# First FFN layer by seven block products in place of eight, with its output stored in DRAM

## Chip, cores and metric

One core of a Trainium2 chip runs the whole program. The metric is the device time of one execution in microseconds, as the median of several runs. The engines are TensorE (PE, matmuls; its weight loads are PEld), VectorE (DVE), ScalarE (ACT), GpSimd (POOL) and SyncE (SP, which issues most transfers). Sixteen DMA engines move the data.

## What is computed

One layer of a hybrid encoder for 1024 prompt tokens and 8 × 16 sample tokens, 1152 rows of 1024 in all. Three mixers come first; the change touches only the end of the layer:

```python
def _merge_and_ffn(x, o_a, o_b, o_c, gate_logits, w_out, ln1_g, ln1_b, w_ff1, b_ff1, w_ff2, b_ff2, ln2_g, ln2_b):
    ...
    h = _layer_norm(DN_ALPHA * x + merged @ w_out, ln1_g, ln1_b)
    f = jnp.square(jax.nn.relu(h @ w_ff1 + b_ff1)) @ w_ff2 + b_ff2
    return _layer_norm(DN_ALPHA * h + f, ln2_g, ln2_b)
```

`w_ff1` is 1024 × 4096 and `w_ff2` 4096 × 1024, all in float32.

## The kernel before

Every float32 product is made of three matmuls: each operand is split into a rounded upper part and the rest (`xh`/`xl` for the activations, `whi`/`wlo` for weights, `uh`/`ul` for the hidden layer, `h2`/`l2`, here also `h`/`l`, for the second weights), and the three products upper × upper, upper × rest and rest × upper are added in PSUM. `split` (L168, L169) makes the two parts: POOL rounds (or ACT, where asked), DVE subtracts. All matmuls are issued at L115.

`phase_out` holds what concerns us. A first loop over nine token tiles of 128 adds the out-projection to the residual, normalises (`layer_norm`, whose last addition of 1024 elements is POOL's, L1319), transposes the result on PE (tile `tp`, PSUM tag t, two banks) and writes it split into `xh` (ACT, L1241) and `xl` (DVE, L1242): feature on the partitions, 8 blocks `k` of 128 features by 1152 tokens. The normalised rows themselves stay in SBUF in nine tiles `acc0` to `acc8`, which later collect the output.

Then the FFN runs in 16 blocks of two hidden tiles `f` of 128. For each `f`, 72 matmuls of 128 × 384 (8 blocks `k`, 3 parts, 3 token chunks) fill PSUM tag g (tile `ps`); ACT takes relu and square (L1263, L1264), and the result is split into `uh` and `ul`, three buffers each. The second layer of the block takes 108 matmuls of 128 × 512 (9 token tiles, 2 halves, 6 each) into tag o (tile `op`, three banks), and DVE adds each bank to its half of an `acc` tile (L1289). After the second block POOL adds the bias `b_ff2` (L1296). The program's order is written as a loop, but a scheduler fixes each engine's own order when the program is built: it puts the first-layer matmuls of one block among the second-layer ones of the block before. At run time each engine works its queue strictly in that order and waits on semaphores. The weights come over SP's queue (`wraw`, `w2raw`).

Of the kernel before, what the change touches and what calls it, by code (L numbers as in the profile page):

```python
# [11 lines left out]
F32 = mybir.dt.float32  # L12
F32R = mybir.dt.float32r
AF = mybir.ActivationFunctionType
ALU = mybir.AluOpType
# [4 lines left out]
P = 128  # L20
D = 1024
# [3 lines left out]
NT = SEQ + DB * DT  # L25
CW = 384
NCH = NT // CW
KT = D // P
MEM = 256
FF = 4096  # L30
NF = FF // P
# [3 lines left out]
ALPHA = 2.0 ** 0.25  # L35
# [22 lines left out]
def run(g, n=-1):  # L58

    while n and next(g, g) is not g:  # L60
        n -= 1


class K:
# [66 lines left out]
    def setup(self):  # L131
        nc, d = self.nc, self.d
        nc.scalar.preload_act_table_set("natural_log_exp_and_others")
        cst = self.const.tile([P, C_END], F32, name="cst")
        self.cst = cst
        self.ident = cst[:, C_ID:C_ID + P]
        self.og = self.dram.tile([KT, P, NT], F32, name="og")
        self.started = set()

        self.gates = [(0, 0), (0, 1), (0, 2), (0, 3), (1, 7)] + [(2, t) for t in range(4)] + [(a, t) for t in range(4, KT) for a in (0, 2)]  # L140
        self.oa, self.oc, self.gb = (self.dram.tile([KT, P, NT], F32, name=n) for n in ("oa", "oc", "gb"))
        self.spq = self.dram.tile([KT, P, NT], F32, name="spq")
        self.spk = self.dram.tile([KT, P, NT], F32, name="spk")
        self.spn = self.dram.tile([2, KT, P, NT], F32, name="spn")
        self.rows = self.dram.tile([2, 8, 9, P], F32, name="rows")
        self.b_dram()
        eps = self.const.tile([P, 4], F32, name="eps")
        nc.vector.memset(eps[:, 0:1], 1e-6)
        nc.vector.memset(eps[:, 1:2], 1e-5)
        nc.vector.memset(eps[:, 2:3], float(np.log(128.0 ** -0.5)))  # L150
        nc.vector.memset(eps[:, 3:4], 1.0)
        self.eps = eps
        self.sums = self.const.tile([P, NT // P, 2], F32, name="sums")
# [1053 lines left out]
    def phase_out(self, pool, ps):  # L1207
        nc, d = self.nc, self.d
        T9 = NT // P
        hh, hl = self.xh, self.xl  # L1210
        accs = [pool.tile([P, D], F32, name=f"acc{i}") for i in range(T9)]
        with self.pool("p2a") as pa:
            for i in range(6):
                nc.scalar.copy(accs[i][:, 0:512], self.early[i])
                nc.sync.dma_start(accs[i][:, 512:D], d["x"][i][:, 512:D])
# [13 lines left out]
            for i in range(T9):  # L1229
# [2 lines left out]
                run(self.out_mm(i, 1, w1, o, accs[i][:, 512:D]))  # L1232
                a = accs[i]
                self.layer_norm(pa, a, self.sums[:, i, :], lng, hl[:, :, t])
                for u in range(2):
                    tp = ps.tile([P, 512], F32, name="tp", tag="t", bufs=2)
                    for k in range(4):
# [4 lines left out]
                    nc.vector.tensor_sub(hl[:, s, t], v, hh[:, s, t].bitcast(F32))  # L1242
        self.right.close()
        with self.pool("p2b") as pb:
            bf = pb.tile([P, NF], F32, name="bf")
            nc.sync.dma_start(bf, d["b_ff1"])
            lng = pb.tile([P, 2, D], F32, name="lng")
            bf2 = pb.tile([P, D], F32, name="bf2")
            for t, n in ((bf2, "b_ff2"), (lng[:, 0, :], "ln2_g"), (lng[:, 1, :], "ln2_b")):
                nc.sync.dma_start(t, d[n].broadcast_to([P, D]))  # L1250
            blk = 2
            for f0 in range(0, NF, blk):
                hid = []
                for f in range(f0, f0 + blk):
                    w = self.weights(d["w_ff1"][f].rearrange("p (k c) -> p k c", k=KT))
                    uh = pb.tile([P, NT], F32R, name="uh", bufs=3)
                    ul = pb.tile([P, NT], F32R, name="ul", bufs=3)
                    for c in range(NCH):
                        n = slice(c * CW, (c + 1) * CW)
                        p = self.psg.tile([P, 512], F32, name="ps", tag="g")  # L1260
                        run(self.gemm(p[:, :CW], w, hh, hl, c * CW, (c + 1) * CW))
                        r = pb.tile([P, CW], F32, name="r", bufs=2)
                        nc.scalar.activation(r, p[:, :CW], AF.Relu, bias=bf[:, f:f + 1])  # L1263
                        nc.scalar.activation(r, r, AF.Square)  # L1264
                        self.split(uh[:, n], ul[:, n], r)
                    w2 = []
                    for u in range(2):
                        raw = pb.tile([P, 512], F32, name="w2raw", bufs=3)
                        nc.sync.dma_start(raw, d["w_ff2"][f][:, u * 512:(u + 1) * 512])
                        h2 = pb.tile([P, 512], F32R, name="h2", bufs=6)  # L1270
                        l2 = pb.tile([P, 512], F32R, name="l2", bufs=6)
                        self.split(h2, l2, raw)
                        w2.append((h2, l2))
                    hid.append((uh, ul, w2))
                last = f0 + blk == NF
                for i in range(T9):
                    t = slice(i * P, (i + 1) * P)
                    for u in range(2):
                        o = ps.tile([P, 512], F32, name="op", tag="o", bufs=3)
                        m = 0  # L1280
                        for uh, ul, w2 in hid:
                            for a, b in ((uh, w2[u][0]), (uh, w2[u][1]), (ul, w2[u][0])):
                                self.mm(o, lhsT=a[:, t], rhs=b, start=m == 0, stop=m == 3 * blk - 1)
                                m += 1
                        a = accs[i][:, u * 512:(u + 1) * 512]
                        if f0 == 0:
                            nc.vector.scalar_tensor_tensor(a, a, ALPHA, o, op0=ALU.mult, op1=ALU.add)
                        elif not last:
                            nc.vector.tensor_add(a, o, a)  # L1289
                        else:  # L1290
                            if u == 0:
                                sm = pb.tile([P, 2], F32, name="sm", bufs=2)
                            nc.vector.tensor_tensor_reduce(out=a, in0=o, in1=a, scale=1.0, scalar=0.0, op0=ALU.add, op1=ALU.add, accum_out=sm[:, u:u + 1])  # L1293
                    a = accs[i]
                    if f0 == blk:
                        nc.gpsimd.tensor_add(a, a, bf2)  # L1296
                    if last:
                        self.layer_norm(pb, a, sm, lng, hl[:, :, t], i >= T9 - 2)
                        m = 2 if i >= T9 - 2 else 1
                        for u in range(m):  # L1300
                            v = slice(u * D // m, (u + 1) * D // m)
                            nc.sync.dma_start(d["o_y"][i][:, v], a[:, v])

    def layer_norm(self, pool, a, s, gb, jk, short=False):

# [99 lines left out]
```

## Time and profile before

| what | value |
|---|---|
| median of 3 runs | 2823.54 us (2819.36 to 2833.57) |
| the profiled execution | 2831.98 us, its span 2830.2 us |
| busy in the span | PE 2685.3, DVE 1460.4, ACT 1008.4, POOL 819.5 us |
| mean granted clock of PE | 0.976 |

The profiled execution is one run among several, and the trace's times are those of that run. Busy is the time in which an engine has an instruction under way; a matmul is shown with its whole pipeline, so that two neighbours overlap, and the distance of two starts is what one costs. The FFN stands from about 2010 us to the end of the span.

### The profile page before, as it was taken

How to read it: one execution, taken by the hardware profiler on the slowest of the kernel's cores; microseconds unless marked ns; L12 is line 12 of the kernel's file. 1: busy time of each engine (PE TensorE's matmuls, PEld its weight loads, DVE VectorE, ACT ScalarE, POOL GpSimd, SP SyncE). 2: the span in 40 equal slices, each digit the busy share in tenths (PEclk: the TensorE clock that was granted, in tenths of full speed). 3: DMA queues.
4: the chain of work that ended last, by engine and by line, in shares of the span. 5: the costliest groups of instructions: out<-in, count | busy, mean ns of one | idle time of the engine just before them, and what ended most of it. 6: DMA issues, size and time to landing. Idle time of an engine off the chain costs nothing.

```text
span 2830.2 us, 45047 instructions
## 1 busy us (share of the span) xinstructions
PE 2685.3 (95%) x16361; PEld 2486.4 (88%) x16361; DVE 1460.4 (52%) x3353; ACT 1008.4 (36%) x2749; POOL 819.5 (29%) x1197
## 2 busy tenths in 40 slices
PE   8989999989899989999989898999999999999997
PEld 7979899989899988998878888888989899998986
DVE  4646474737375655333366557554544444444445
ACT  4636363736364544222423333233411111111113
POOL 2222132212122221122355555432342121121212
PEclk9999999999999999999989999999999999999999
DMA  7252524333333424344676676654201011110101
GB/s 254 76 172 79 174 86 174 119 124 125 121 130 129 155 91 158 136 164 151 189 207 191 192 209 199 189 161 144 71 30 60 30 52 38 38 53 30 52 27 67
DMA packets 263006, 343.27 MB, mean 121 GB/s; under 512 B 54704, under 2 KB 178240, under 8 KB 258752
## 3 DMA queue, kind: packets, MB, share of 16 engines
q1 hardware_dynamic: 201344, 245.93, 27.7%
q10 hardware_dynamic: 61440, 94.46, 9.5%
q8 instruction: 129, 2.11, 0.3%
q14 instruction: 93, 0.76, 0.1%
HBM read 235.18 MB, written 105.13 MB: 120 GB/s over the span
## 4 chain that ended last, share of the span: by engine, by line
PE 51%; DMA 8%; DVE 4%; issue 3%; POOL 1%; ACT 1%; SPq 0%; DVEq 0%; ACTq 0%; POOLq 0%
PE ps L115 26%; PE op L115 15%; PE t L115 3%; PE S L115 1%; PE sc L115 1%; PE kk L115 1%; DMA wraw<-in_w_mem 1%; DVE tmp L775 1%; PE o L115 1%; PE tb L120 1%; DMA bv<-spn 1%; PE ob L115 1%; PE od L115 1%; DMA o_akp<-y 1%; DMA og<-gt 1%
## 5 line engine op out<-in xcount | busy, mean ns | idle before, releaser
L115 PE MATMUL ps<-xh,whi 128*128 128x384 f32 x2712 | 958.1, 353 | 31.4 <-ACT y L313 13.9
L115 PE MATMUL ps<-xl,whi 128*128 128x384 f32 x2712 | 935.6, 345 | 0.0
L115 PE MATMUL ps<-xh,wlo 128*128 128x384 f32 x2712 | 933.5, 344 | 0.9 <-DVE wlo L169 0.9
L115 PEld LDWEIGHTS ps<-xh,whi 128*128 128x128 f32 x2712 | 517.7, 191 | 50.3 <-ACT y L313 14.5
L115 PEld LDWEIGHTS ps<-xl,whi 128*128 128x128 f32 x2712 | 517.4, 191 | 14.1 <-issue 2.9
L115 PEld LDWEIGHTS ps<-xh,wlo 128*128 128x128 f32 x2712 | 515.9, 190 | 10.2 <-issue 3.9
L168 POOL TENSOR_SCALAR whi<-wraw 128x512 fp32r<-128x512 f32 x261 | 180.6, 692 | 513.6 <-PE ps L115 414.8
L1289 DVE TENSOR_TENSOR acc<-op,acc 128x512 f32<-128x512 f32 x252 | 174.2, 691 | 276.1 <-PE op L115 276.0
L1263 ACT ACTIVATE r<-ps,bf 128x384 f32<-128x384 f32 x96 | 55.7, 581 | 664.7 <-PE ps L115 664.7
L169 DVE TENSOR_TENSOR wlo<-wraw,whi 128x512 fp32r<-128x512 f32 x261 | 195.2, 748 | 185.0 <-POOL whi L168 179.0
L115 PE MATMUL op<-h,uh 128*128 128x512 f32 x576 | 225.6, 392 | 1.2 <-DVE sm L1293 1.2
L115 PE MATMUL op<-h,ul 128*128 128x512 f32 x576 | 226.1, 392 | 0.0
L115 PE MATMUL op<-l,uh 128*128 128x512 f32 x576 | 225.5, 392 | 0.0
L371 POOL TENSOR_SCALAR pt<-pt,sta 128x640 f32<-128x640 f32 (+3 forms) x144 | 114.1, 793 | 293.5 <-DVE sta L370 242.5
L168 POOL TENSOR_SCALAR uh<-r 128x384 fp32r<-128x384 f32 x96 | 55.5, 578 | 492.0 <-ACT r L1264 480.1
L367 DVE CUSTOM_DVE_ANT_0 pt<-S,tab 128x640 f32<-128x640 f32 (+4 forms) x128 | 83.9, 656 | 122.8 <-PE S L115 85.6
L607 DVE SCALAR_TENSOR_TENSOR y<-z,wc,y 128x384 f32<-128x384 f32 (+1 forms) x216 | 128.7, 596 | 17.5 <-ACT y L604 15.5
L115 PEld LDWEIGHTS op<-h,ul 128*128 128x128 f32 x576 | 108.2, 188 | 23.9
L115 PEld LDWEIGHTS op<-h,uh 128*128 128x128 f32 x576 | 108.2, 188 | 19.5 <-DVE sm L1293 2.0
L115 PEld LDWEIGHTS op<-l,uh 128*128 128x128 f32 x576 | 108.1, 188 | 15.5
L369 ACT ACTIVATE pt<-pt,sta 128x640 f32<-128x640 f32 (+3 forms) x144 | 101.4, 705 | 49.4 <-DVE sta L368 35.7
L169 DVE TENSOR_TENSOR ul<-r,uh 128x384 fp32r<-128x384 f32 x96 | 53.7, 560 | 102.2 <-POOL uh L168 102.2
(374 smaller groups left out, 4600.5 us busy)
## 6 DMA issues: line engine op xcount, KB each, us to landing
wraw<-in_w_in SPq DMA_DIRECT2D x160, 256.0 KB
kb<-in_cak SPq DMA_DIRECT2D x16, 1024.0 KB
vb<-in_cav SPq DMA_DIRECT2D x16, 1024.0 KB
o_aks<-kb ACTq DMA_DIRECT2D x16, 1024.0 KB
wraw<-in_w_ff SPq DMA_DIRECT2D x64, 256.0 KB
w2raw<-in_w_ff SPq DMA_DIRECT2D x64, 256.0 KB
o_avs<-vb ACTq DMA_DIRECT2D x16, 992.0 KB
spn<-kn ACTq DMA_DIRECT2D x48, 192.0 KB
```

The lines of the kernel that those rows point to most:

```text
L115: ins = self.nc.tensor.matmul(out, **kw)
L120: ins = self.nc.tensor.transpose(out, **kw)
L168: nc.gpsimd.tensor_scalar(hi, raw, 1.0, 0.0, op0=ALU.mult, op1=ALU.add)
L169: nc.vector.tensor_sub(lo, raw, hi.bitcast(F32))
L367: nc.vector.tensor_tensor_reduce(out=P_, in0=S, in1=tab, scale=1.0, scalar=-3e38, op0=ALU.add, op1=ALU.max, accum_out=st[:, 0:1])
L369: nc.scalar.activation(P_, P_, AF.Exp, bias=st[:, 1:2], accum_out=st[:, 2:3])
L371: nc.gpsimd.tensor_scalar(P_, P_, st[:, 3:4], 0.0, op0=ALU.mult, op1=ALU.add)
L607: nc.vector.scalar_tensor_tensor(y[:, :w], z[:, i:i + w], wc[:, i:i + 1], y[:, :w], op0=ALU.mult, op1=ALU.add)
L775: nc.vector.tensor_tensor(tmp[:, 0:t, 0:t], y[:, 0:t, 0:t], m[:, 0:t, t].unsqueeze(1).broadcast_to([72, t, t]), op=ALU.mult)
L1263: nc.scalar.activation(r, p[:, :CW], AF.Relu, bias=bf[:, f:f + 1])
L1289: nc.vector.tensor_add(a, o, a)
```

## The change

The first layer is written as a 2 × 2 block product, h cut into two halves of features and two of tokens, and `w_ff1` into two halves of features and two neighbouring tiles `f`. One level of the Strassen–Winograd scheme takes seven products in place of eight. Its operands on the activation side are four sums (S1, S2, S4 in new tiles `s1h` to `s4l`; S3 over the part of `xh`/`xl` that is no longer wanted), made once after the first loop; on the weight side four sums per pair of tiles (`tsum`, on POOL). The seven results are put together by DVE adds into tiles `keep`. The tiles f = 0 and 1 are still done directly, with 384 columns; the 15 pairs after them have matmuls of 288 columns, 24 per product.

The hidden layer goes to a DRAM buffer `hid`, the normalised rows to `hd`, and the second layer is a loop of its own, `ffn2`, which reads both back. It does its rounding to `uh` on ACT.

```diff
@@ phase_out
-        accs = [pool.tile([P, D], F32, name=f"acc{i}") for i in range(T9)]
         with self.pool("p2a") as pa:
+            accs = [pa.tile([P, D], F32, name=f"acc{i}") for i in range(T9)]
...
                 self.layer_norm(pa, a, self.sums[:, i, :], lng, hl[:, :, t])
+                nc.scalar.dma_start(self.hd[i], a)
...
         with self.pool("p2b") as pb:
...
+            self.ffn1(pb, ps)
+        with self.pool("p2c") as pb:
+            self.ffn2(pb, ps)
+
+    def ffn1(self, pool, ps):
...
+        S = [tuple(pool.tile([P, 4, H], F32R, name=f"s{i}{n}") for n in "hl") for i in (1, 2, 4)]
+        S.insert(2, (hh[:, top, two], hl[:, top, two]))
+        for k in range(4):
...
+            tmp = lambda: pool.tile([P, H], F32, name="sum", bufs=5)
+            s1, s2, s3, u, v = (tmp() for _ in range(5))
+            nc.vector.tensor_add(s1, a21[0], a22[0])
+            nc.gpsimd.tensor_add(u, a21[1], a22[1])
+            nc.vector.tensor_add(s1, s1, u)
+            nc.gpsimd.tensor_sub(s3, a11[0], a21[0])
+            nc.gpsimd.tensor_sub(v, a11[1], a21[1])
+            nc.vector.tensor_add(s3, s3, v)
+            nc.vector.tensor_sub(s2, s1, a11[0])
+            nc.vector.tensor_sub(s2, s2, a11[1])
+            self.cast(S[0], k, s1)
+            self.cast(S[2], k, s3)
+            self.cast(S[1], k, s2)
+            nc.vector.tensor_sub(s2, a12[0], s2)
+            nc.vector.tensor_add(s2, s2, a12[1])
+            self.cast(S[3], k, s2)
...
+        for f in range(2, NF, 2):
...
+            t1, t2, t3, t4 = (pool.tile([P, 4, P], F32, name="tsum", bufs=6) for _ in range(4))
+            nc.gpsimd.tensor_sub(t1, R[0, 1], R[0, 0])
+            nc.gpsimd.tensor_sub(t2, R[1, 1], t1)
+            nc.gpsimd.tensor_sub(t3, R[1, 1], R[0, 1])
+            nc.gpsimd.tensor_sub(t4, R[1, 0], t2)
...
+            names = iter("tgotgot")
+            def product(a, raw):
+                w = [self.wp.tile([P, 4, P], F32R, name=n, tag=n, bufs=4) for n in ("whi", "wlo")]
+                self.split(*w, raw)
+                tag = next(names)
...
+                    for k in range(4):
+                        for m, (x, y) in enumerate(((0, 0), (0, 1), (1, 0))):
+                            self.mm(banks[j], lhsT=w[x][:, k, :], rhs=a[y][:, k, half(j)], start=k == m == 0, stop=k == 3 and m == 2)
...
+            for j, b in enumerate(product(A11, R[0, 0])):
+                nc.scalar.copy(p1[:, half(j)], b)
+            hidden(add(p1, product(A12, R[1, 0])), 0, one)
+            u2 = add(p1, product(S[1], t2))
+            u3 = add(u2, product(S[2], t3))
+            b = product(S[0], t1)
+            u4 = add(u2, b)
+            hidden(add(u3, b), 1, two)
+            hidden(add(u3, product(A22, t4)), 0, two)
+            hidden(add(u4, product(S[3], R[1, 1])), 1, one)
+
+    def cast(self, pair, k, src):
+        self.nc.scalar.copy(pair[0][:, k, :], src)
+        self.nc.vector.tensor_sub(pair[1][:, k, :], src, pair[0][:, k, :].bitcast(F32))
+
+    def ffn2(self, pb, ps):
...
+                raw = pb.tile([P, NT], F32, name="uraw", bufs=2)
+                nc.sync.dma_start(raw, self.hid[f])
+                uh = pb.tile([P, NT], F32R, name="uh", bufs=3)
+                ul = pb.tile([P, NT], F32R, name="ul", bufs=3)
+                for c in range(NCH):
+                    n = slice(c * CW, (c + 1) * CW)
+                    self.split(uh[:, n], ul[:, n], raw[:, n], "act")
...
+            if f0 == 0:
+                for i in range(T9):
+                    nc.sync.dma_start(accs[i], self.hd[i])
```

`hidden` takes relu and square of a `keep` tile on ACT (576 elements) and sends it to `hid` over ACT's queue; `add` makes a new `keep` tile from two PSUM banks of 288 and an older one, on DVE; `half(j)` is a half of 288 columns. The matmuls, adds and bias of the second layer are those of before.

Three places of the engines' queues. First DVE, just after the last tile of the first loop. Before (`acc_21010` is the ninth token tile), the lower parts of the hidden chunks and of the weights follow on the last `xl`:

```order
L1310 SCALAR_TENSOR_TENSOR acc_21010<-acc_21010,lst,lng 128x1024
L1242 TENSOR_TENSOR xl<-tp,xh 128x4x128 x4
L169 TENSOR_TENSOR ul<-r,uh 128x384
L1242 TENSOR_TENSOR xl<-tp,xh 128x4x128 x2
L169 TENSOR_TENSOR ul<-r,uh 128x384
L169 TENSOR_TENSOR l_21707<-w2raw,h_21706 128x512
L169 TENSOR_TENSOR l_21713<-w2raw,h_21712 128x512
```

Now (the rows carry the changed kernel's lines: 1280 to 1292 are the sums, 1355 the lower part in `cast`, 171 that in `split`):

```order
L1424 SCALAR_TENSOR_TENSOR acc_21015<-acc_21015,lst,lng 128x1024
L1245 TENSOR_TENSOR xl<-tp,xh 128x4x128 x6
L1280 TENSOR_TENSOR sum<-xh 128x576
L1282 TENSOR_TENSOR sum<-sum 128x576
L1286 TENSOR_TENSOR sum<-sum,xh 128x576
L1280 TENSOR_TENSOR sum<-xh 128x576
L1287 TENSOR_TENSOR sum<-sum,xl 128x576
L1355 TENSOR_TENSOR s1l<-sum,s1h 128x576
L1285 TENSOR_TENSOR sum<-sum 128x576
L1355 TENSOR_TENSOR s2l<-sum,s2h 128x576
L171 TENSOR_TENSOR wlo<-raw,whi 128x512
L1291 TENSOR_TENSOR sum<-xh,sum 128x576
```

The sums of all four `k` stand there in one piece, 44 sums and lower parts among which the weights' lower parts (`wlo`) for the first products are spread, and the hidden chunks' `ul` are gone from this place.

Second DVE again, at the border of two blocks of the second layer. Before, from the last add of one block (`acc_21010`) to the first of the next (`acc_21002`), the operands are for matmuls of the first layer that PE has in between:

```order
L1289 TENSOR_TENSOR acc_21010<-op,acc_21010 128x512
L169 TENSOR_TENSOR l_23220<-w2raw,h_23219 128x512
L169 TENSOR_TENSOR l_23226<-w2raw,h_23225 128x512
L169 TENSOR_TENSOR wlo<-wraw,whi 128x512
L169 TENSOR_TENSOR ul<-r,uh 128x384 x3
L169 TENSOR_TENSOR wlo<-wraw,whi 128x512 x2
L1289 TENSOR_TENSOR acc_21002<-op,acc_21002 128x512
L169 TENSOR_TENSOR ul<-r,uh 128x384
```

Now, with `acc_25844` the ninth and `acc_25836` the first token tile:

```order
L1403 TENSOR_TENSOR acc_25844<-op,acc_25844 128x512
L171 TENSOR_TENSOR l_27031<-w2raw,h_27030 128x512
L171 TENSOR_TENSOR l_27037<-w2raw,h_27036 128x512
L171 TENSOR_TENSOR ul<-uraw,uh 128x384
L1403 TENSOR_TENSOR acc_25844<-op,acc_25844 128x512
L171 TENSOR_TENSOR l_27197<-w2raw,h_27196 128x512
L171 TENSOR_TENSOR ul<-uraw,uh 128x384 x5
L1403 TENSOR_TENSOR acc_25836<-op,acc_25836 128x512 x2
```

Six lower parts of the hidden layer now stand together at the border, five of them between the last add of the old block and the first add of the new one.

Third SP, where the first layer ends and the second begins (`uraw` is the hidden tile read back, `acc` the nine reloaded tiles). There was no such place before:

```order
L1369 DMA uraw<-hid 128x1152
L1378 DMA w2raw<-in_w_ff 128x512 x2
L1369 DMA uraw<-hid 128x1152
L1378 DMA w2raw<-in_w_ff 128x512
L1386 DMA acc_25836<-hd 128x1024
L1386 DMA acc_25837<-hd 128x1024
L1386 DMA acc_25838<-hd 128x1024
L1386 DMA acc_25839<-hd 128x1024
L1386 DMA acc_25840<-hd 128x1024
L1386 DMA acc_25841<-hd 128x1024
L1386 DMA acc_25842<-hd 128x1024
L1378 DMA w2raw<-in_w_ff 128x512
```

The fourth `w2raw`, the second half of the weights of f = 1, comes behind seven of the nine `acc` tiles.

## Rows read from the trace of the kernel before

**Rows 1.** The page: busy time per engine, and the largest group of weight loads.

```profile
PE 2685.3 (95%) x16361; PEld 2486.4 (88%) x16361; DVE 1460.4 (52%) x3353; ACT 1008.4 (36%) x2749; POOL 819.5 (29%) x1197
...
L115 PEld LDWEIGHTS ps<-xh,whi 128*128 128x128 f32 x2712 | 517.7, 191 | 50.3 <-ACT y L313 14.5
```

**Rows 2.** Windows over the FFN: busy us per engine, PE's clock, DMA share, GB/s.

```profile
core 0: us, PE busy (x) PEld busy (x) DVE busy (x) ACT busy (x) POOL busy (x), PEclk, DMA share, GB/s
...
2010.00:2830.00 820.00, 804.50 (x4040) 730.61 (x4038) 374.88 (x555) 131.75 (x244) 192.09 (x237) 0.99 0.14 47
...
2200.00:2300.00 100.00, 100.00 (x503) 90.99 (x503) 43.93 (x64) 13.27 (x24) 19.30 (x28) 1.00 0.13 43
```

**Rows 3.** PE's timeline at three places: start, duration, instruction.

```profile
2223.25 0.34 PE L115 MATMUL ps<-xh,whi 128*128 128x384 f32 x1
...
2229.96 0.34 PE L115 MATMUL ps<-xh,wlo 128*128 128x384 f32 x1
...
1142.49 0.28 PE L115 MATMUL ps<-memh,whi 128*128 128x256 f32 x1
...
1147.18 0.28 PE L115 MATMUL ps<-meml,whi 128*128 128x256 f32 x1
...
2205.69 0.40 PE L115 MATMUL op<-h,uh 128*128 128x512 f32 x1
...
2207.53 0.40 PE L115 MATMUL op<-h,ul 128*128 128x512 f32 x1
```

**Rows 4.** Groups by line and shape, 2020 to 2830 us: busy, mean ns | idle before.

```profile
L1289 DVE TENSOR_TENSOR acc<-op,acc 128x512 f32<-128x512 f32 x252 | 174.2, 691 | 276.1 <-PE op L115 276.0
...
L169 DVE TENSOR_TENSOR ul<-r,uh 128x384 fp32r<-128x384 f32 x95 | 53.1, 560 | 101.3 <-POOL uh L168 101.3
...
L1296 POOL TENSOR_TENSOR acc<-acc,bf 128x1024 f32<-128x1024 f32 x9 | 22.0, 2446 | 13.1 <-DVE acc L1289 13.1
...
L1264 ACT ACTIVATE r<-r 128x384 f32<-128x384 f32 x94 | 49.2, 525 | 2.9
```

**Rows 5.** POOL's groups by line and shape over the span, two-operand ones.

```profile
L853 POOL TENSOR_TENSOR am<-at,cst 128x384 f32<-128x384 f32 x48 | 51.6, 1075 | 54.6 <-PE t L115 37.7 <-issue 15.5 <-DMA at<-dat 0.8
...
L980 POOL TENSOR_TENSOR we<-wv,cst 128x512 f32<-128x512 f32 x16 | 18.2, 1135 | 3.8 <-ACT wv L968 3.3 <-PE kk L115 0.5
```

**Rows 6.** Timelines of POOL and of DVE around 2121 to 2129 us.

```profile
2121.42 1.20 POOL L168 TENSOR_SCALAR h<-w2raw 128x512 fp32r<-128x512 f32 x2
2122.59 1.09 POOL L168 TENSOR_SCALAR whi<-wraw 128x512 fp32r<-128x512 f32 x1
2123.66 1.04 POOL L168 TENSOR_SCALAR h<-w2raw 128x512 fp32r<-128x512 f32 x1
2124.67 2.81 POOL L1296 TENSOR_TENSOR acc<-acc,bf 128x1024 f32<-128x1024 f32 x1
...
2121.91 0.69 DVE L1289 TENSOR_TENSOR acc<-op,acc 128x512 f32<-128x512 f32 x1 [1.21 <-PE op L115]
2122.52 1.70 DVE L169 TENSOR_TENSOR l<-w2raw,h 128x512 fp32r<-128x512 f32 x2
2124.15 1.09 DVE L169 TENSOR_TENSOR wlo<-wraw,whi 128x512 fp32r<-128x512 f32 x1
2125.16 2.87 DVE L169 TENSOR_TENSOR l<-w2raw,h 128x512 fp32r<-128x512 f32 x1
```

**Rows 7.** Windows, a loaded one and one in the LN1 loop: DMA share and GB/s.

```profile
1925.00:1930.00 5.00, 5.00 (x22) 4.05 (x23) 2.21 (x4) 2.05 (x3) 0.00 (x0) 1.00 1.04 388
...
1960.00:1970.00 10.00, 10.00 (x46) 8.29 (x45) 4.04 (x6) 5.40 (x10) 3.48 (x2) 1.00 0.00 0
```

**Rows 8.** Timeline where the first loop ends: PE's last transposes, DVE's last lower parts.

```profile
2017.51 1.03 PE L120 MATMUL tp<-cst,acc 128*128 128x128 f32 x8
...
2019.14 1.40 DVE L1242 TENSOR_TENSOR xl<-tp,xh 128x512 fp32r<-128x512 f32 x2
```

**Rows 9.** PE's timeline after two gaps, the gap and its releaser in brackets.

```profile
1529.48 0.49 PE L115 MATMUL sc<-bv,Y 128*128 128x128 f32 x2 [1.73 <-DVE S L941]
...
869.84 0.55 PE L120 MATMUL pvt<-cst,y 128*128 128x128 f32 x3 [2.14 <-ACT y L338]
```

**Rows 10.** Windows of 6 us after these two gaps.

```profile
1531.00:1537.00 6.00, 6.00 (x21) 4.97 (x22) 3.59 (x17) 0.09 (x1) 0.74 (x2) 0.50 0.43 137
871.00:877.00 6.00, 6.00 (x38) 5.97 (x37) 3.39 (x10) 1.90 (x7) 1.24 (x2) 1.00 0.46 169
```

More of the change, by code (lines that the diff above doesn't have):

```diff
@@ L141, in setup @@
         self.oa, self.oc, self.gb = (self.dram.tile([KT, P, NT], F32, name=n) for n in ("oa", "oc", "gb"))
+        self.hd = self.dram.tile([NT // P, P, D], F32, name="hd")
+        self.hid = self.dram.tile([NF, P, NT], F32, name="hid")
         self.spq = self.dram.tile([KT, P, NT], F32, name="spq")
@@ L1244, in phase_out @@
         with self.pool("p2b") as pb:
[L1245 to L1275, printed above, removed]
-                for i in range(T9):
[L1277 to L1302, printed above, removed]
```

94 lines of the change are left out of this document (added).

## The prediction

> **What bounds the kernel now.** I read the page first: TensorE is busy 95% of the span [rows 1]. The windows over the FFN come next: from 2010 us to the end PE is busy 804.5 of 820 us, in its middle 100% at the full clock, while DVE has 44%, ACT 13%, POOL 19% and the DMA engines 13% [rows 2]. So in this stage only two things count: the time of a matmul, and any wait that the change puts ahead of PE. Everything else has room, unless it stands in a queue at the wrong moment. The PE timeline then gives the price of a matmul as the distance of starts: 384 columns, 38 steps from 2223.25 to 2229.96, 176.6 ns; 256 columns, 40 steps from 1142.49 to 1147.18, 117.3 ns; 512 columns, 8 steps from 2205.69 to 2207.53, 230 ns [rows 3]. A weight load lasts 191 ns on the page [rows 1], longer than the 117.3 ns at 256 columns, and does not set the distance there.
>
> **The change part by part. The matmuls.** 288 columns do not occur before. Between the 256 and the 384 row a straight line gives 117.3 + 32/128 × 59.3 = 132.1 ns. A pair of f tiles had 2 × 72 × 176.6 ns = 25.43 us and now has 7 × 24 × 132.1 ns = 22.19 us. Fifteen pairs: 15 × 3.24 = **48.6 us less** (the tiles f = 0 and 1 stay direct, FFN2 keeps its 1728 matmuls). The bounds: if the distance did not fall below 256's line at all beyond what the 384 row scales to (132.5 ns), 47.6; if the weight load set it (191 ns), each pair would take 32.1 us and the change would lose 100. The 256-column rows speak against the latter.
>
> The Trainium skill ("TensorE: Matmul & The Clock Gate", Back-to-back issue gap) gives N/2.4 + 2.5 ns for one matmul alone. By it 384 columns take 162.5 ns and 288 take 122.5 ns, and the gain would be 42.3 us, an estimate from that page; the trace's 176.6 ns differs from it, so the rows stand.
>
> **Inside a pair.** In 22.2 us DVE gets 14 adds of 288 from PSUM and 7 lower parts of 512: an add of 512 takes 0.69 us and a lower part of 384 takes 0.56 [rows 4], which is about 0.46 for 288, so 6.4 + 7 × 0.75 = 11.7 us. POOL gets 4 subtractions (1.14 for 512 columns) and 7 roundings at 0.60 [rows 5, 6], 8.8 us; ACT 8 activations of 576 at 0.7 and two copies, under 8 us (0.525 for 384, [rows 4]). DMA moves 1.05 MB of weights in and 1.18 MB of hidden out, 100 GB/s where 388 has been reached [rows 7]. All hidden under PE. The seventh product's banks (tag t) are the first ones of the next pair; its first half ends 1.6 us before it is wanted again, and the add takes 0.46 us. I count 0, with up to 1 us each (15) on the high side.
>
> **The operand sums.** Right after the last LN1 tile DVE gets 44 operations of 576 elements and POOL 12. Up to the lower half of S2's fourth block (the fiftieth DVE row of this piece) DVE runs 41 of these, 7 weight parts and 2 adds. Ahead of the same point POOL runs its 12 sums, 8 weight sums and 7 roundings. PE has as cover what stands between the last transposes and the matmul that reads that block: 96 direct matmuls and 128 product matmuls, 96 × 0.1766 + 128 × 0.1321 = 33.9 us.
>
> The two engines do not run side by side here. The timeline at 2121 shows it: with 2.32 left of a POOL addition, DVE's l takes 2.87 us instead of 0.69; and from 2122.52 to 2128.03, in 5.51 us, four DVE operations (0.53 each at 512 elements, what remains without their start-up) and three POOL ones (0.6, 0.6 and 2.4 alone, less start-up) have run one after the other [rows 6]. An addition that reads PSUM is not held: the one at 2121.91 takes its 0.69 beside POOL [rows 6]. All 44 sums read SBUF on both sides. So the occupied times add: DVE 41 × 0.60 + 7 × 0.53 + 0.7 = 29 us (576/512 of 0.53 is 0.60), POOL 12 × 1.35 + 8 × 1.1 + 7 × 0.55 = 29 us (1.08 at 384 and 1.14 at 512 elements [rows 5]). Together 58 us. DVE begins this at about 2020.5, when its last xl operation of before ends, PE's cover at 2018.5 [rows 8]. PE then waits 58 − 33.9 + 2 = 26 us; with full durations instead of occupied time (DVE 36, POOL 31) it is 35. I take **31 us**, the middle. The Trainium skill ("SBUF — State Buffer", Who interferes with whom) has this as an exclusive claim for a whole instruction, by which 35 would be the number; the 5.51 us above are shorter than that. The lower bound, if they overlapped freely, is DVE's own 36 us against 33.9: about 4 to 6 us.
>
> **From FFN1 to FFN2.** The reload of the hidden layer shares SBUF with FFN1's tiles, so its first transfer leaves when FFN1's last matmul has ended. On SP's queue there are, ahead of the fourth w2raw: two uraw (0.59 MB each), three w2raw (0.26) and seven acc (0.52), 5.6 MB, and 0.6 MB of hidden writes still going out. At 388 GB/s [rows 7] that is 16 us, and with rounding and lower part the operand is there after 18.7 us. PE can run 27 matmuls (6.2 us) without it. **12.5 us idle**, and the clock: 2.5 more, so **15** (11 to 20).
>
> **Block boundaries of FFN2.** Before, PE had FFN1's 72 matmuls of the next tiles between two FFN2 blocks, and the operands of the next block were made under them. Now block follows block. uh/ul have three buffers, a block holds two, so the next block's second tile and the one after it are made only when the old block's last matmul has ended (E). DVE's queue then holds: lower part c0 of the second tile, the add of acc8's second half, an l2, two more lower parts, three of the tile after it (each behind its ACT cast, 0.51 us apart), and only behind all these the first add of the new block, acc0. Starting at about E + 1.0 (cast, l2 parts held by POOL's roundings), 6 lower parts of 384 at 0.47, l2 and two adds at 0.6 each make acc0's add end at about E + 5.7 to 6.4. PE has three banks: 18 matmuls × 0.23 = 4.13 us, then it waits for acc0. **About 2.0 us per boundary** (1.2 to 3.1). In the trace a PE gap of 1.73 us was followed by 6 us at a granted clock of 0.50, half of full (1.2 of 2.4 GHz), one of 2.14 us by 6 us at 1.00 [rows 9, 10]. Six us at half clock lose 3. With one boundary in three I add 1.0. Fifteen boundaries: 15 × 3.0 = **45 us** (15 × 1.2 = 18 to 15 × 5 = 75). At the boundary after the second block POOL also has nine additions of 2.45 us [rows 4] beside the lower parts: **3 us** (0 to 8).
>
> **Edits at no cost.** The nine hd writes leave in the LN1 loop, where DMA stands at 0 GB/s and ACT has half its time free [rows 7]; if that cover were gone, 9 × 0.52 MB would cost 12 us. The hidden writes lie under the pairs, as above. FFN2's own loads are 2.2 MB per block of 24.8 us. The tail after the last FFN2 block is the same code.
>
> **Sum.** −48.6 + 31 + 15 + 45 + 3 = +45 us. The profiled execution took 2832.0 us (span 2830.2), 8.4 above the median of the runs, 2823.5. On the profile that makes 2877, on the median 2869, rounded **2870**.
>
> **The rivals.** A, *the gain shows* (other side): DVE and POOL overlap in the operand sums and PE finds its operands after 5 us, and at the boundaries acc0's add ends before PE's third bank is full. It decides at the first: operands done 34 us after the last transposes. Then −48.6 + 5 + 13 + 15 × 0.5 = −23, about **2800**. For it: the free-running bound above; against it: the 2.87 us row. B, *near cancel*: the sums cost 25, the transition 11, each boundary 1.0 us without a slower clock: −48.6 + 25 + 11 + 15 = +2, about **2826**. For it: the gap of 2.14 us after which the clock stayed. C, *each boundary drops the clock*: 15 × 5 = 75 in place of 45, with 3 more at the sums: about **2902**; the 1.73 us row speaks for it. D, *288 columns cost what the weight load lasts* (191 ns): +100 in place of −48.6, about 3020; the 256-column rows rule it out nearly.
>
> **How the numbers follow.** A measurement of this kernel can tell about 0.5%, 14 us, from no change. My case (sums 25 to 37, boundaries 1.2 to 3.5 us) 0.56, its own range 2840 to 2900; A 0.12; B 0.16; C 0.13; D 0.03. Faster is A, 0.12 (below 2809); same is B and a little of mine, 0.18; slower 0.70. The range leaves out A's lower half, D and the upper third of C: 2806 to 2915.
>
> **What would show it.** In the windows after 2020 us: PE busy falls for some 30 us while DVE and POOL are both near full, and DVE's sums take more than 0.76 us (576/0.96 + 0.16) each; if PE stays at 100%, the step is wrong. In a pair: starts of 288-column matmuls 132 ns apart, a pair in 22.2 us. At the end of FFN1: PE idle for 10 to 15 us with DMA near 390 GB/s and h2 of f = 1 last. At FFN2's boundaries: PE idle about 2 us every 27 us, released by the add of acc0, some followed by a clock of 0.50. I am wrong if the boundaries cost under 0.7 us each, or if the pairs wait for DVE.

## The result, and the profile after

| | before | changed |
|---|---|---|
| median | 2825.7 us (4 runs) | 2859.3 us (4 runs) |
| ratio | | 1.0124, 95% interval 1.0106 to 1.0143 |
| span of the profiled execution | 2830.2 us | 2856.5 us |
| PE busy | 2685.3 us | 2653.5 us |
| DVE / POOL busy | 1460.4 / 819.5 us | 1620.3 / 898.2 us |

The change is slower by 33.6 us. PE is busy for 31.8 us less and waits for more than that. Where it waits is seen in the windows of the changed kernel (columns as in [rows 2]):

```profile
core 0: us, PE busy (x) PEld busy (x) DVE busy (x) ACT busy (x) POOL busy (x), PEclk, DMA share, GB/s
2010.00:2060.00 50.00, 34.47 (x187) 31.94 (x186) 49.90 (x43) 13.63 (x24) 37.08 (x24) 0.83 0.12 43
2060.00:2070.00 10.00, 5.70 (x24) 4.65 (x22) 9.46 (x15) 2.01 (x3) 5.46 (x5) 0.63 0.15 52
...
2200.00:2300.00 100.00, 100.00 (x756) 100.00 (x755) 50.04 (x96) 30.92 (x46) 47.58 (x51) 1.00 0.29 104
...
2400.00:2410.00 10.00, 6.76 (x21) 4.46 (x21) 2.67 (x4) 0.00 (x0) 0.62 (x1) 0.84 1.01 385
...
2600.00:2700.00 100.00, 92.45 (x397) 75.05 (x396) 65.65 (x103) 7.76 (x18) 10.39 (x13) 0.98 0.26 85
```

Four places, four patterns. To 2070: PE waits and runs at a lower granted clock (0.83, then 0.63), DVE is full, POOL is busy for three quarters and then for half of the time. At 2200: the products, PE full at full clock, 756 matmuls in 100 us, 132.3 ns each. At 2400: PE waits and DMA is full. At 2600: PE has lost 7.5%, and no engine nor DMA is full, which points to a loss of order, not of work.

**The operand sums.** DVE's and POOL's timeline in that stage (start, duration):

```profile
2015.53 1.98 DVE L1355 TENSOR_TENSOR s2l<-sum,s2h 128x576 fp32r<-128x576 f32 x1
2017.44 1.77 DVE L171 TENSOR_TENSOR wlo<-raw,whi 128x512 fp32r<-128x512 f32 x1
2019.13 1.84 DVE L1291 TENSOR_TENSOR sum<-xh,sum 128x576 f32<-128x576 f32 x1
...
2032.46 0.76 DVE L1355 TENSOR_TENSOR s2l<-sum,s2h 128x576 fp32r<-128x576 f32 x1
...
2063.25 0.74 DVE L1355 TENSOR_TENSOR s2l<-sum,s2h 128x576 fp32r<-128x576 f32 x1
```

```profile
2015.02 1.88 POOL L1281 TENSOR_TENSOR sum<-xl 128x576 f32<-128x576 f32 x1 [0.69 <-DVE s1l L1355]
2016.86 1.80 POOL L1304 TENSOR_TENSOR tsum<-raw,tsum 128x512 f32<-128x512 f32 x1
2018.62 1.74 POOL L1305 TENSOR_TENSOR tsum<-raw 128x512 f32<-128x512 f32 x1
```

The same operation of DVE takes 0.76 us where POOL is idle and 1.8 to 2.0 where POOL adds; POOL's addition of 576 takes 1.43 where it starts while DVE waits (2007.07) and 1.9 here. The two take turns, as in [rows 6]. The last lower part that PE needs (2063.25, the fourth `s2l`) ends at 2064.0, 59 us after the first sum begins.

PE's waits in that stage (2003 to 2080 us: total, times, longest), the longest of them, and the first matmul that reads the last block of `s2l`:

```profile
PE ps L115 <- ACT r L1269: 8.4, 4, 5.0
PE tp L115 <- DVE wlo L171: 3.5, 1, 3.5
PE ps L115 <- DVE keep L1332: 3.1, 2, 1.9
```

```profile
2034.52 0.61 PE L115 MATMUL ps<-xh,whi 128*128 128x288 f32 x1 [5.01 <-ACT r L1269]
...
2064.51 0.44 PE L115 MATMUL op<-s2l,whi 128*128 128x288 f32 x1
```

PE does not stand still until the last sum is there: it waits in small pieces, 20.9 us in all, and what it does in between runs slower.

**The change of layers.** The first layer's last matmul ends at 2387.05. PE's gaps, POOL's rounding and SP's queue after it:

```profile
2393.07 0.79 PE L115 MATMUL op<-h,uh 128*128 128x512 f32 x1 [5.86 <-POOL h L170]
2395.26 1.22 PE L115 MATMUL op<-h,uh 128*128 128x512 f32 x2 [1.40 <-POOL h L170]
...
2407.74 1.65 PE L115 MATMUL op<-h,uh 128*128 128x512 f32 x3 [2.15 <-POOL h L170]
```

```profile
2407.06 0.62 POOL L170 TENSOR_SCALAR h<-w2raw 128x512 fp32r<-128x512 f32 x1 [9.07 <-DMA w2raw<-in_w_ff]
```

```profile
2389.61 9.24 SPq L1386 DMA_DIRECT2D acc<-hd  x7
2398.95 0.72 SPq L1378 DMA_DIRECT2D w2raw<-in_w_ff  x1
```

The fourth `w2raw` is issued only after seven `acc`, and its rounding begins 20.0 us after the first layer's end. PE's gaps up to there, two small ones behind `acc` among them, sum to 10.5 us, and its clock is low in between (windows as above):

```profile
2392.00:2397.00 5.00, 2.53 (x5) 1.74 (x6) 2.76 (x6) 0.89 (x3) 1.42 (x2) 0.50 0.98 361
...
2407.00:2412.00 5.00, 4.26 (x13) 3.42 (x13) 2.33 (x4) 0.00 (x0) 0.62 (x1) 0.66 1.04 407
```

**A block border**, here the one at 2492 (DVE's timeline, then PE's first matmul behind the gap):

```profile
2489.14 0.68 DVE L1403 TENSOR_TENSOR acc<-op,acc 128x512 f32<-128x512 f32 x1
2489.74 0.68 DVE L171 TENSOR_TENSOR l<-w2raw,h 128x512 fp32r<-128x512 f32 x1
2490.34 2.84 DVE L171 TENSOR_TENSOR ul<-uraw,uh 128x384 fp32r<-128x384 f32 x5
2493.10 1.28 DVE L1403 TENSOR_TENSOR acc<-op,acc 128x512 f32<-128x512 f32 x2
```

```profile
2493.84 0.50 PE L115 MATMUL op<-h,uh 128*128 128x512 f32 x1 [1.99 <-DVE acc L1403]
```

Five lower parts and an `l` stand between the last add of the old block and the first of the new one; PE has filled its third bank and waits 1.99 us. PE's waits over the second layer, summed by releaser, put this first:

```profile
PE op L115 <- DVE acc L1403: 25.8, 14, 2.0
PE op L115 <- POOL h L170: 9.4, 3, 5.9
PE op L115 <- DVE l L171: 3.2, 1, 3.2
```

After some borders the clock falls, after others not (windows of 6 us behind two of these gaps of 1.99):

```profile
2493.84:2499.84 6.00, 6.00 (x26) 4.98 (x27) 3.99 (x7) 0.00 (x0) 0.00 (x0) 1.00 0.59 194
...
2574.18:2580.18 6.00, 6.00 (x19) 4.81 (x20) 3.12 (x5) 0.00 (x0) 0.00 (x0) 0.72 0.64 199
```

Of the 14 borders from 2434 on (twelve gaps of 1.99, one of 1.57, one of 3.18), six show 0.72, and there PE does some 19 matmuls in place of 26: 7 × 0.23 = 1.6 us each. The fifteenth border, ahead of the last block, has no gap.

**The account.** From PE's timeline three moments can be read for each kernel: the end of the last transposes, of the first layer's last matmul and of the second layer's last one. Before, the layers are interleaved and only the sum exists.

| kernel | last transposes end | first layer | second layer | both |
|---|---|---|---|---|
| before | 2018.5 | | | 797.4 |
| changed | 2003.7 | 383.4 | 454.5 | 837.9 |
| sums on DVE | 2009.6 | 372.9 | 452.2 | 825.1 |
| four direct tiles | 2015.7 | 370.6 | 452.6 | 823.2 |
| four direct, seven banks | 2011.2 | 369.4 | 451.5 | 820.9 |
| four slots, 8 h2/l2 | 2014.7 | 383.5 | 416.4 | 799.9 |
| 8 h2/l2 alone | 2014.2 | 383.7 | 453.8 | 837.5 |
| four w2raw | 2012.3 | 383.0 | 454.2 | 837.2 |
| all direct, no products | 2006.9 | 399.8 | 450.5 | 850.3 |
| all remedies | 2017.5 | 356.6 | 427.4 | 784.0 |
| all but w2raw | 2016.5 | 356.6 | 416.3 | 772.9 |
| the same, second time | 2017.8 | 356.6 | 416.5 | 773.1 |
| all but w2raw, late loads | 2019.6 | 356.6 | 414.5 | 771.1 |

In the changed kernel the matmuls alone are 96 × 0.1766 + 2520 × 0.1323 = 350.4 us in the first layer, so 33.0 us are lost there. Ahead of the matmul at 2064.51 stand 224 of them, 33.9 us of work; it starts 60.9 us after the last transposes, so 27.0 are lost up to it and 6.0 after it. By kind, 20.9 of the 33.0 are PE's gaps, and the other 12.1 are mostly matmuls at the lower clock.

In the second layer a block of 108 matmuls that has no gap takes 24.5 us (seen with four slots, below), 227 ns for each, a little less than the 230 of [rows 3]. Sixteen such blocks are 392.0 us, so 62.5 of the 454.5 are lost. The second block's first matmul starts at 2427.64, 40.6 us after the first layer's end: 16.1 lost at the change of layers. The blocks two to fifteen take 387.3 us together, 44.3 more than 14 × 24.5: the borders. The last block takes 2.2 more; it does so with four slots too, so this is no border's loss. A border with a gap of 1.99 and a full clock costs 2.3 us, one with the slower clock 3.9, and the one after the second block, where POOL adds the bias, 7.1.

Against before this makes −48.1 (15 pairs of 25.43 − 22.22) − 5.4 (1728 matmuls of 512 columns, 392.0 in place of 397.4) + 33.0 + 16.1 + 44.3 + 2.2 = +42.1; before lost 1.6 in the same stretch itself (797.4 less 2256 × 0.1766 + 397.4) and the tail grew by 0.7, so +41.2; measured 852.9 − 811.7 = +41.2 from the last transposes to the end of the span.

The stretch ahead of it does the same work in all these kernels, and it ended between 2003.7 and 2019.6 us: it scatters by 16 us among executions. The two profiled executions lie at its lower end and near its upper one, which is why the spans differ by 26.3 only. Within a kernel the stretch behind is steadier (the first layer took 356.6 us in all four executions of the last four rows), so the experiments are read from the account first and from the ratio second.

### The profile page after: what moved, and what is told of

It is laid out like the page before. It is cut to its first block, busy times and chain, and to the rows that moved or that the text cites. A ratio compares the mean times of both kernels' runs of the same rounds, so it can differ in the third digit from the quotient of the medians.

```text
span 2856.5 us, 46556 instructions
## 1 busy us (share of the span) xinstructions
PE 2653.5 (93%) x16721; PEld 2445.5 (86%) x16721; DVE 1620.3 (57%) x3652; ACT 1060.4 (37%) x2831; POOL 898.2 (31%) x1218
## 4 chain that ended last, share of the span: by engine, by line
PE 48%; DVE 9%; DMA 7%; issue 3%; ACT 1%; POOL 1%; SPq 0%; DVEq 0%; ACTq 0%; POOLq 0%
PE ps L115 17%; PE op L115 16%; PE tp L115 5%; PE t L115 2%; DVE ul L171 1%; DMA bv<-spn 1%; PE S L115 1%; DVE tmp L777 1%; PE kk L115 1%; PE sc L115 1%; PE o L115 1%; PE tb L120 1%; PE od L115 1%; ACT uh L166 1%; DMA o_akp<-y 1%
## 5 line engine op out<-in xcount | busy, mean ns | idle before, releaser
L115 PE MATMUL ps<-xh,whi 128*128 128x384 f32 (+2 forms) x2112 | 748.0, 354 | 38.9 <-ACT y L315 14.2
L115 PE MATMUL ps<-xl,whi 128*128 128x384 f32 (+2 forms) x2112 | 725.1, 343 | 0.0
L115 PE MATMUL ps<-xh,wlo 128*128 128x384 f32 (+2 forms) x2112 | 723.6, 343 | 1.3 <-DVE wlo L171 1.3
L115 PEld LDWEIGHTS ps<-xh,whi 128*128 128x128 f32 (+1 forms) x2112 | 402.9, 191 | 52.3 <-ACT y L315 14.8
L115 PEld LDWEIGHTS ps<-xl,whi 128*128 128x128 f32 (+1 forms) x2112 | 403.2, 191 | 6.8 <-issue 2.9
L115 PEld LDWEIGHTS ps<-xh,wlo 128*128 128x128 f32 (+1 forms) x2112 | 402.1, 190 | 8.0 <-issue 3.9
L170 POOL TENSOR_SCALAR whi<-wraw 128x512 fp32r<-128x512 f32 x201 | 132.6, 660 | 477.5 <-PE ps L115 386.0
L171 DVE TENSOR_TENSOR wlo<-wraw,whi 128x512 fp32r<-128x512 f32 x201 | 143.0, 712 | 151.3 <-POOL whi L170 147.6
L170 POOL TENSOR_SCALAR h<-w2raw 128x512 fp32r<-128x512 f32 x64 | 50.3, 787 | 362.3 <-DVE acc L1403 256.9
L1336 ACT ACTIVATE keep<-keep,bf 128x576 f32<-128x576 f32 x60 | 46.7, 779 | 188.5 <-DVE keep L1332 188.5
```

The lines of the kernel that those rows point to most:

```text
L115: ins = self.nc.tensor.matmul(out, **kw)
L170: nc.gpsimd.tensor_scalar(hi, raw, 1.0, 0.0, op0=ALU.mult, op1=ALU.add)
L171: nc.vector.tensor_sub(lo, raw, hi.bitcast(F32))
L1336: nc.scalar.activation(r, r, AF.Relu, bias=bf[:, f + g:f + g + 1])
```

## The experiments

Ratios are to the kernel before, run on the same chip in the same hours.

**Sums on DVE.** Does the operand stage last long because two engines take turns, or because DVE has too much?

```diff
-            nc.gpsimd.tensor_add(u, a21[1], a22[1])
+            nc.vector.tensor_add(u, a21[1], a22[1])
-            nc.gpsimd.tensor_sub(s3, a11[0], a21[0])
-            nc.gpsimd.tensor_sub(v, a11[1], a21[1])
+            nc.vector.tensor_sub(s3, a11[0], a21[0])
+            nc.vector.tensor_sub(v, a11[1], a21[1])
```

> The twelve sums of POOL in the operand stage go to DVE, nothing else changes. Theory (DVE and POOL take turns there, so their times add): each moved sum costs 0.67 us on DVE in place of 1.38 on POOL, so the stage gets 12 x 0.7 = 8 us shorter; the changed kernel's 2859 becomes about 2851, and DVE's 576-element sums show 1.8 us less often. Rival (the engines run side by side and DVE alone is late): DVE has 12 x 0.67 = 8 us more to do, about 2867.

Measured 2858.8 us, ratio 1.0106 (1.0092 to 1.0121); the first layer 372.9 us, 10.5 less. DVE got twelve more operations and was done sooner: from the first sum to the end of the fourth `s2l` 51.9 us in place of 59, 7 less where 8 was expected. Its groups by shape (2004 to 2075 us, busy and mean ns), one of the same line in the changed kernel and here:

```profile
L1292 DVE TENSOR_TENSOR sum<-sum,xl 128x576 f32<-128x576 f32 x4 | 5.6, 1390 | 0.0
```

```profile
L1292 DVE TENSOR_TENSOR sum<-sum,xl 128x576 f32<-128x576 f32 x4 | 3.7, 923 | 0.0
...
L1284 DVE TENSOR_TENSOR sum<-xl 128x576 f32<-128x576 f32 x4 | 3.0, 748 | 0.0
```

The theory of turns holds; the end-to-end time does not resolve it, the account does.

**Four direct tiles.** Is it cover that lacks?

```diff
-        for f in range(2):
+        for f in range(4):
...
-        for f in range(2, NF, 2):
+        for f in range(4, NF, 2):
```

> Four hidden tiles are done directly in place of two, fourteen pairs follow. Theory (the operand stage is late because PE has only 34 us of work for its 59): 25 us more cover; the pair given up costs 3.2 us, the lost time of 33.6 us in the first layer falls to 4 to 8, so about 2859 - 28 + 3 = 2834. Rival (the loss is tied to the start of the products, not to cover): it moves along with them and the time is 2862.

Measured 2852.0 us, ratio 1.0076 (1.0064 to 1.0088); the first layer 370.6 us. The direction is right, the size is half: 12.8 us in place of 25. PE's gaps there are of another kind:

```profile
2027.14 0.44 PE L115 MATMUL ps<-xh,whi 128*128 128x384 f32 x1 [1.49 <-ACT r L1269]
2038.93 0.41 PE L115 MATMUL ps<-xh,whi 128*128 128x384 f32 x1 [3.05 <-ACT r L1269]
```

The direct tiles' relu stands in ACT's queue behind casts of sums that DVE has not made yet, and PE waits for the bank. In the changed kernel there is such a gap too, of 5.01 us at 2034. That led to the next.

Two things that the expectation held fixed have changed. Ahead of the first matmul that waits for the fourth `s2l` (at 2080.66) PE now has 240 direct and 60 product matmuls in place of 96 and 128, so the cover is 50.3 us, 16 more and not 25. And from the first sum to the end of that `s2l` it takes 63.5 us in place of 59.

**Four direct tiles, seven banks.**

```diff
-                p = self.psg.tile([P, 512], F32, name="ps", tag="g")
+                tag = "gto"[c]
+                p = self.psg.tile([P, 512], F32, name="ps", tag="g") if tag == "g" else ps.tile([P, 512], F32, name=tag + "p", tag=tag, bufs={"t": 2, "o": 3}[tag])
```

> As the kernel with four direct tiles, and the direct tiles' results go to the seven PSUM banks of tags g, t and o in turn in place of the two of g. Theory (what was left there, 9.3 us of gaps, is PE waiting for a bank that ACT has not emptied, since relu stands in ACT's queue behind the casts of sums that DVE has not made): these gaps vanish, the first layer takes 362 us in place of 370.6, the whole about 2843. Rival (PE would only wait the same time later, for the sums themselves): 370 and 2852.

Measured 2856.0 us, ratio 1.0105 (1.0084 to 1.0126); the first layer 369.4 us. The rival was right: the gaps behind ACT's relu are gone, and PE waits nearly as long, 10.3 us in all in place of 11.4, now mostly at the next things: 4.7 at the lower part of a weight, 3.1 at the cast of `s2` and 2.2 at its lower part. The longest:

```profile
2036.47 0.44 PE L115 MATMUL ps<-xh,wlo 128*128 128x384 f32 x1 [4.01 <-DVE wlo L171]
```

The queue of ACT only decided where the wait showed. With four direct tiles the stage is longer and fewer products stand ahead of its end, in both kernels (here 62.6 us, with the same 60 products ahead). That it is longer because the weights of the direct tiles need DVE and POOL as well, in the same queues, fits, but was not tried by itself.

**Four slots.** The borders.

```diff
-                uh = pb.tile([P, NT], F32R, name="uh", bufs=3)
-                ul = pb.tile([P, NT], F32R, name="ul", bufs=3)
+                uh, ul = self.xh[:, f % 4, :], self.xh[:, 4 + f % 4, :]
...
-                    h2 = pb.tile([P, 512], F32R, name="h2", bufs=6)
-                    l2 = pb.tile([P, 512], F32R, name="l2", bufs=6)
+                    h2 = pb.tile([P, 512], F32R, name="h2", bufs=8)
+                    l2 = pb.tile([P, 512], F32R, name="l2", bufs=8)
```

> In the second layer the hidden tiles lie in four slots of xh (freed part by part) in place of three buffers each, and h2/l2 have eight buffers. Theory (1.99 us per block border because six lower parts stand ahead of acc0's add, plus the slower clock that some of these gaps bring): the gaps at 15 borders fall under 0.5 us each, no stretch at a clock of 0.50 follows, the second layer loses about 35 us less: 2824. Rival (the three PSUM banks alone make the gap, through the add of acc0): unchanged, 2859.

Measured 2829.2 us, ratio 0.9992 (0.9980 to 1.0005); the second layer 416.4 us, 38.1 less. Between the borders' adds one lower part is left, the others stand further on among the new block's adds (DVE's timeline), and PE has no gap here (two are left, of 1.6 and 1.9 us, where POOL adds the bias):

```profile
2495.57 0.68 DVE L1402 TENSOR_TENSOR acc<-op,acc 128x512 f32<-128x512 f32 x1
2496.17 0.68 DVE L171 TENSOR_TENSOR l<-w2raw,h 128x512 fp32r<-128x512 f32 x1
2496.77 0.55 DVE L171 TENSOR_TENSOR xh<-uraw,xh 128x384 fp32r<-128x384 f32 x1
2497.24 1.28 DVE L1402 TENSOR_TENSOR acc<-op,acc 128x512 f32<-128x512 f32 x2
```

```profile
2600.00:2700.00 100.00, 100.00 (x443) 82.56 (x442) 71.84 (x115) 12.89 (x25) 11.99 (x16) 1.00 0.27 91
```

**Eight h2/l2 alone**, the last four lines of that diff.

> Of the kernel with four slots only the eight h2/l2 buffers are kept, the hidden tiles have three buffers as in the changed kernel. Theory (the hidden tiles' buffers make the gap at each border): 1.99 us at each border as before, 2859, ratio to the kernel before 1.012. Rival (the second weights were what was late): the gaps go, 2825, ratio 1.000.

Measured 2864.3 us, ratio 1.0140 (1.0108 to 1.0171); the borders keep their 1.99 us, the second layer is 453.8. So the hidden tiles' buffers are needed. Whether the four slots would do it without the eight h2/l2, and whether it is the fourth place or the freeing part by part that counts, was not run.

**Four w2raw buffers.** The change of layers.

```diff
-                    raw = pb.tile([P, 512], F32, name="w2raw", bufs=3)
+                    raw = pb.tile([P, 512], F32, name="w2raw", bufs=4)
```

> w2raw gets four buffers, so that the fourth one is sent ahead of the nine acc tiles at the change from first to second layer. Theory (the fourth w2raw lies behind 3.7 MB of acc tiles): the block's first operand set is complete about 9 us after the last matmul of the first layer in place of 20; the first block's loss of 17 us falls to 8 or 9, about 2850. Rival (the transition is paid for the hidden tiles' way through DRAM and for the acc tiles themselves): no change, 2859.

Measured 2871.2 us, ratio 1.0140 (1.0127 to 1.0154); the second layer 454.2 us, as long as without. PE runs without a gap from 10.1 us after the first layer's end, as the theory had it, but the second block starts only 3.8 us sooner, not 8 or 9. This was given back: 2.4 us in the second block and 1.1 over the twelve blocks from the fourth on, at whose borders the gap is 2.5 us, twelve times alike:

```profile
2528.76 0.50 PE L115 MATMUL op<-h,uh 128*128 128x512 f32 x1 [2.51 <-DVE acc L1403]
```

One more buffer also changed the order on DVE: between the last add of a block and the first of the next stand two `l` in place of one.

**All direct.** What do the products bring on their own?

> The first layer is done directly for all 32 hidden tiles, without sums and products; its output still goes through DRAM and the second layer is that of the changed kernel. Theory (the products save 3.2 us in each of 15 pairs and the sums cost 33.6 of it): the first layer takes 48 us more for its matmuls and loses 30 less, so 401 us from the last transposes in place of 383, and the whole 2859 + 18 = 2877. Rival (the products gain nothing, all that was lost lies in the first layer): 2825, the time of the kernel before.

It runs the direct loop over all `f` and leaves out the sums and the pairs. Measured 2875.1 us, ratio 1.0168 (1.0151 to 1.0185); the first layer 399.8 us. Both are as the theory had them. So of the 48.1 us that the products save 16.4 arrive, and the second layer as a loop of its own, fed through DRAM, by itself costs 850.3 − 797.4 = 53 us.

**All remedies**, with and without the fourth `w2raw`: four direct tiles on seven banks, sums on DVE, four slots, eight h2/l2.

> All remedies together: four direct tiles on seven banks, the twelve sums on DVE, hidden tiles in four slots of xh, eight h2/l2 and four w2raw buffers. If the losses are separate they add: the first layer about 355 us, the second 408 to 412, so 2012 + 355 + 410 + 14 = 2791, 1.2% faster than before. If one takes the place of another: about 2815.

> As all remedies together, with three w2raw buffers. If the fourth buffer helps at the change of layers once the borders no longer wait: 5 us slower than with it, 2796; if its half microsecond per border (seen where it was tried alone) remains: 3 us faster than with it.

With it 2816.3 us, ratio 0.9958 (0.9944 to 0.9973); without it 2805.2 us, 0.9922 (0.9902 to 0.9942). Together the remedies of the first layer give 356.6 us, 3.0 above the matmuls' own 353.6 (240 × 0.1766 + 2352 × 0.1323). The whole came to the second figure of the first expectation, where one loss takes the place of another. In the second layer the fourth buffer costs 11.1 us: the direction of the second expectation's last case, with nearly four times its 3 us. They are lost at the borders. With the fourth buffer twelve of them keep a gap of 0.61 to 0.63 us, and each of these blocks takes 25.5 us in place of 24.5, 12.1 in all; there too two `l` stand ahead of the first add (DVE's timeline, then PE's first matmul behind the gap):

```profile
2549.41 0.68 DVE L171 TENSOR_TENSOR l<-w2raw,h 128x512 fp32r<-128x512 f32 x1
2550.01 1.87 DVE L1403 TENSOR_TENSOR acc<-op,acc 128x512 f32<-128x512 f32 x3
...
2550.74 0.50 PE L115 MATMUL op<-h,xh 128*128 128x512 f32 x1 [0.61 <-DVE acc L1403]
```

At the change of layers it gains 0.9 us. The windows of the kernel that has it, 20 and 40 us after the first layer's end, show why so little:

```profile
2394.00:2399.00 5.00, 5.00 (x24) 4.14 (x23) 2.33 (x4) 0.00 (x0) 0.00 (x0) 1.00 1.04 390
...
2414.00:2419.00 5.00, 2.46 (x11) 2.04 (x12) 5.00 (x9) 1.34 (x3) 2.40 (x3) 1.00 0.92 303
```

DMA is full for 25 us with either order (shares of 0.94 to 1.04 in the windows from 5 us on); with the fourth buffer the first block is 7.6 us shorter and the second, whose operands come late and together, 6.7 longer, with DVE full at its border and PE half idle. With either order the third block starts after 66 to 67 us. That what has to be brought bounds the stretch fits this.

The kernel without it was run a second time:

> The fastest combination so far once more, beside the other on the same chip: ratio to the kernel before 0.992 (0.990 to 0.994).

2807.8 us, ratio 0.9924 (0.9902 to 0.9947).

**Late loads.**

```diff
...
+            if f0 == 4:
                 for t, n in ((bf2, "b_ff2"), (lng[:, 0, :], "ln2_g"), (lng[:, 1, :], "ln2_b")):
...
-                if f0 == blk:
+                if f0 == 4 * blk:
                     nc.gpsimd.tensor_add(a, a, bf2)
```

> The fastest combination so far (three w2raw buffers), with the loads of b_ff2 and the LN2 vectors (1.5 MB) behind the second block's operands in SP's queue and POOL's nine bias additions in the fifth block in place of the second. Theory (the change of layers is bound by what DMA has to bring, and the second block's border by POOL's additions): 2 to 4 us for the loads, and the gaps of 1.6 and 1.85 us after the second block move into the fifth: 2 to 5 us faster than that combination, ratio 0.991. Rival (the additions cost the same wherever they stand and the loads are off the path): same as it, 0.992.

2803.6 us, ratio 0.9914 (0.9887 to 0.9940); the second layer 414.5 us, 1.8 to 2.0 less than the two executions without. The two gaps moved behind the fifth block and kept their size, so the rival was right on the additions; what was gained lies ahead of the third block, at the lower end of the 2 to 4 us expected of the loads:

```profile
2519.79 0.50 PE L115 MATMUL op<-h,xh 128*128 128x512 f32 x1 [1.60 <-DVE acc L1404]
```

End to end it cannot be told from the kernel without late loads.

## Why the prediction was right, point by point

**Matmuls.** 132.1 ns forecast, 132.3 measured; −48.6 forecast, −48.1 measured. Rival D is out. Not foreseen was that the second layer's matmuls of 512 columns, charged as before, would cost 227 ns in place of 230, 5.4 us less in all. By the formula of the Trainium skill for one matmul alone ("TensorE: Matmul & The Clock Gate", Back-to-back issue gap) 288 columns would take 122.5 ns, an estimate from that page; the trace does not agree.

**Inside a pair.** Nothing forecast, nothing seen: PE is at 100% and full clock from 2080 to 2300.

**Operand sums.** +31 forecast, +33.0 measured; the stage was to be 58 us long and took 59. That DVE and POOL take turns is shown by the kernel with the sums on DVE. The number for PE is near in part by luck. The forecast was a wait alone, 26 by occupied times or 35 by full durations, and took the middle. Measured are 27.0 us up to the matmul that needs the last `s2l`, close to the figure by occupied times, and 6.0 after it, of which 2.5 are a wait for a DVE add (`keep`) and the rest mostly the lower clock. The clock was no term of this forecast, and PE stood idle for 20.9 us, not 31. Rival A needed the operands 34 us after the last transposes and fell. Not foreseen was also that a part of the wait would show at ACT's relu; that it was the same wait in another place is shown by the seven banks.

The Trainium skill ("SBUF — State Buffer", Who interferes with whom) says that an operation of DVE with two inputs in SBUF and a GpSimd operation that reads SBUF contend for a shared port pair, which is an exclusive lock. The trace agrees in that DVE's operation takes 1.8 to 2.0 us there in place of 0.76; the two together are done in less than the 0.76 + 1.43 that full durations in turn would take.

**Change of layers.** +15 forecast, +16.1 measured, the last operand's rounding begun 20.0 us after the first layer's end, where 18.7 was forecast for the operand. Of the sum 12.5 was to be idle and 2.5 the clock; idle were 10.5, and the other 5.6 are mostly the clock, at 0.50 to 0.66. The theory of the four w2raw, that the loss hangs on one transfer in the wrong place, did not hold: with that transfer ahead the second block started only 3.8 us sooner, and as much was lost again behind it.

**Borders.** A gap of 2.0 us forecast, 1.99 measured at twelve of 14; 48 forecast with the bias additions, 44.3 measured. Of fifteen borders 14 have a gap. The clock's part was over-sized: one in three at 3.0 us was forecast, 1.0 each; six of 14 at 1.6 us is 0.7. The prediction gives no working for one in three; it was a guess between its two rows. In the traces of the five other kernels with gaps of 1.99 us three to five of thirteen were followed by the slower clock. The bias additions, 3 forecast, are the 3.2 us by which their border costs more than another with the slower clock. That the place of the hidden tiles makes the gap is shown by the four slots, and by the eight h2/l2 that alone change nothing. Rival C's price was not reached.

**Sum.** +45 forecast, +41.2 in the traces from the last transposes on, +33.6 between the medians. The prediction stood on a profiled execution whose stretch ahead of the change had ended near the upper end of its scatter; I took 8.4 us off for that. Whether the rest, 7.6 us between the traces and the medians, is that scatter too is not settled. It fits that the eight h2/l2 alone and the four w2raw, whose stretch behind is as long as the changed kernel's (837.5 and 837.2 us), stand 34.8 and 40.3 us above the kernel before by their medians.

## What to carry to other kernels

Fewer operations on the engine that bounds are worth what is left after the work that feeds them is placed: here 48 us saved, 33 of them lost again to sums made in one piece on two engines that hold each other up, while 14 pairs in place of 15, with the sums on one engine, two more direct tiles ahead and seven banks for them, lost 3. A wait of the engine that bounds can also cost clock: in the first layer 20.9 of the 33.0 us were idle, the rest mostly slower matmuls. When a loop that was interleaved with another is made to stand alone, its buffers have to reach past a block's end: look for what stands in a queue between the last instruction of one round and the first of the next. With this in order nearly the same change is 0.8% faster than before.

## What the runs showed of the hardware

The length of a gap alone did not tell whether PE's clock would fall. In the changed kernel five of twelve gaps of 1.99 us (and the one of 3.18) were followed by a granted clock of 0.72 over 6 us, that is a part at half speed; in the kernel with four w2raw one of thirteen gaps of 2.5 us was, the first, and none of the other twelve:

```profile
2556.13:2562.13 6.00, 6.00 (x26) 4.99 (x27) 3.44 (x6) 0.00 (x0) 0.00 (x0) 1.00 0.52 190
```

What decides it was not tried. So the half microsecond more of that kernel's gaps was mostly made up by the clock: its twelve blocks from the fourth on took 1.1 us more in all.
